# A written list of steps in place of a clock: the order of recurrence and attention in a hybrid diffusion block

## The chip, the cores and the metric

One core of a Trainium2 chip runs one launch of the kernel. The metric is the device time of that launch in microseconds (us); for the kernel before, the median of three runs is 1243.65 us (1242.34 to 1245.85). Five engines matter below: TensorE (PE), VectorE (DVE), ScalarE (ACT), SyncE (SP, which issues the DMAs here) and GpSimd (POOL, nearly unused). Each works through its own instructions in order.

## The reference

One layer over 256 latent and 256 context tokens, 2048 wide, all in float32. Cut to what matters here:

```python
u_x = split_in((rmsnorm(x, norm_w) * (1 + sc_x) + sh_x) @ w_in)      # 10,048 columns; ctx likewise
r, v, kk, decay, a, k_mod = rwkv_prepare(...)                         # per token, two directions, 16 heads of 64

def rwkv7_step(S, xs):                                                # over 256 ctx tokens, then 256 latent ones
    r, w, k, v, kk, akk = xs
    sa = jnp.einsum("dbhij,dbhj->dbhi", S, -kk)
    S = S * w[..., None, :] + sa[..., :, None] * akk[..., None, :] + v[..., :, None] * k[..., None, :]
    return S, jnp.einsum("dbhij,dbhj->dbhi", S, r)

o_rw_x = rwkv_finish(...)                                             # group norm, bonus, silu gate
att_x = blocked_attend(q_x, concat([k_x, k_c]), concat([v_x, v_c]))   # 8 heads, 512 keys, softmax
o_ml_x = att_x * jax.nn.silu(zm_x)
x_new = x + g_x * ((g_r * (o_rw_x @ w_branch_rwkv) + g_m * (o_ml_x @ w_branch_mla)) @ w_out)
```

## The kernel before, in words

**Stages.** First the modulation and the normalised inputs, held for the whole kernel as two halves `hmh` and `hml` (a float32 number as a rounded part and its rest). Then the *recurrence*: the 16 heads are taken as 8 pairs `p`; every pair has a context half and a latent half, so 16 halves, worked in 9 groups of one or two. The 512 tokens are cut into chunks of 64. Then the *attention* over four pairs of heads, then the two branch projections and the output projection.

**Filler.** The projections of `w_in` that the recurrence does not need at once (merge gates, attention's q, k, v, gates, later pairs' columns) are *filler*: `background()` gives them out in pieces. A piece of one weight block loads 256 KB (`w`, by SP, four buffers), rounds it on ACT (`wh`, a CAST of 128x512), takes the rest on DVE (`wl`, a TENSOR_TENSOR of 128x512) and multiplies both into the PSUM tile `acc`: for the 256 latent tokens 12 matmuls per piece, for all 512 tokens a piece is half a block. `wh` has three buffers, `wl` two.

**Chains.** Beside the filler run four kinds of generators, which stop at each `yield`:
- the front chain (`unit_keys`, `front`, `front2`): decays, keys, and the chunk matrices `AQ` and `AR`;
- one `diagonal` per half, the lane that inverts the 16x16 diagonal blocks: `AQ` goes to DRAM (`dl`), comes back in another layout (`ln`, a DMA), is copied to `wt`, inverted there by 14 pairs of instructions on DVE (`pr`, `wt`), goes out to `dw` and comes back as `WT`;
- the back chain (`back`): four rounds of block products (`lev`, PSUM tile `lv`) that make `W2`, then four steps over the chunks, each of three bursts on PE with a copy by DVE or ACT after each: `px` (copied to `xs`), `pu` (copied to `UV`), and the state's update `pm` (`Mn`);
- `final`: group norm, bonus and gate of a finished pair.

**Who sets the order.** `drive` calls the next generator by a clock: the wrappers `Tensor` and `Elementwise` add up an estimate of each instruction's time, and a chain goes on when its estimated results are there (`LF`, `FX`, and the five waits `LT` of a lane) and PE's estimated load over the last `WIN` is at least `DENS`; where no chain is due, a piece of filler comes. In the attention a loop over six stages advances all generators in turn and adds `BG0` = 8 pieces of filler per round in the first stage and `BGM` = 1.3 later. The instructions in that order are then given to a list scheduler, which orders each engine's queue by that order and by priorities: `HP` for the rounding of weights, `HS` for the inversion, `HB` for the tail of a burst on PE.

**Stores.** Finished projections are copied or activated into an SBUF tile `th` and stored to DRAM by SP (`thd`, `zmd`, `kvd`, `qdd`, `krd`), 50 of them, on the queue that also issues the weight loads.

Of the kernel before, what the change touches and what calls it, by code (L numbers as in the profile page):

```python
# [53 lines left out]
HP, HS, HB = 500, 300, 600  # L54
# [3 lines left out]
LF = 0.4  # L58
LATX = 0.0
FX = 2.0  # L60
LT = (3.5, 5.0, 2.0, 4.5, 5.5)
PD = CH * CH + CH

WIN, DENS = 3.0, 0.7
M1 = 24

BG0, BGM = 8, 1.3


class Clock:  # L70

    def __init__(self):
        self.t = 0.0
        self.ready = 0.0
        self.log = []

    def density(self, window):

        while self.log and self.log[0][0] < self.t - window:
            self.log.pop(0)
        return sum(c for _, c in self.log) / window / 1000


class Tensor:


    def __init__(self, engine, clock):
        self.engine, self.clock = engine, clock  # L90

    def add(self, us, columns):
        c = self.clock
        c.t = c.ready = c.t + us
        c.log.append((c.t, columns))
# [10 lines left out]
    def matmul(self, out, lhsT, rhs, **kw):  # L106
        n, k, m = math.prod(rhs.shape[1:]), lhsT.shape[0], math.prod(lhsT.shape[1:])
        if lhsT.dtype == F32R:
            self.add((max(256, n) / 2400 + 0.003) * k / 128, n * k / 128)
        elif m <= 64:  # L110
            self.add(n / 1200 + 0.044, 2 * n * k / 128)
        else:
            self.add((max(512, 4 * n) / 2400 + 0.005) * max(k, 64) / 128, 2 * n * k / 128)
        if self.head is None:
            return self.engine.matmul(out, lhsT=lhsT, rhs=rhs, **kw)  # L115
        if len(self.head) < self.heads:
            self.head.append(self.engine.matmul(out, lhsT=lhsT, rhs=rhs, **kw))  # L117
            return self.head[-1]
        with self.tc.high_priority(HB):
            i = self.engine.matmul(out, lhsT=lhsT, rhs=rhs, **kw)  # L120
            for h in self.head:
                self.tc.add_manual_dep(i.ins, h.ins.name, BEHIND, reason="burst")
        return i

    def transpose(self, *a):
        self.add(0.13, 0)
        return self.engine.transpose(*a)  # L127


class Elementwise:  # L130


    def __init__(self, engine, clock, rate, fixed):
        self.engine, self.clock, self.rate, self.fixed, self.t = engine, clock, rate, fixed, 0.0

    def __getattr__(self, name):
        fn = getattr(self.engine, name)

        def call(out, *a, **kw):
            c = self.clock  # L140
            c.ready = self.t = max(self.t, c.ready) + math.prod(out.shape[1:]) / self.rate + self.fixed
            return fn(out, *a, **kw)  # L142
        return call
# [3 lines left out]
def hybrid_block(  # L147
# [20 lines left out]
    nc = tc.nc  # L168
    clock = Clock()
    V, S = Elementwise(nc.vector, clock, 960, 0.066), Elementwise(nc.scalar, clock, 1200, 0.08)  # L170
    E = Tensor(nc.tensor, clock)
# [300 lines left out]
    def merge_gate_g(i):  # L472

        ps = yield from proj_g(40 + i, T)
        th = wp.tile([P, T], F32, name="th", tag="th", bufs=2)
        S.activation(th, ps, AF.Tanh, scale=0.5)
        nc.sync.dma_start(thd[i], th)
# [8 lines left out]
    def zm_g(i):  # L486

        ps = yield from proj_g(16 + i, T)
        th = wp.tile([P, T], F32, name="th", tag="th", bufs=2)
        S.activation(th, ps, AF.Tanh, scale=0.5)  # L490
        V.scalar_tensor_tensor(th, th, 1.0, ps, ALU.add, ALU.mult)
        nc.sync.dma_start(zmd[i], th)
        done.add(("zm", i))
# [3 lines left out]
    def spill(dst, ps, col):  # L497

        th = wp.tile([P, T], F32, name="th", tag="th", bufs=2)
        n = dst.shape[0]  # L500
        S.copy(th[0:n], ps)
        nc.sync.dma_start(dst, th[0:n])
        sq = wp.tile([P, T], F32, name="th", tag="th", bufs=2)
        S.activation(sq[0:n], ps, AF.Square)
        yield
        pss = pp.tile([P, 512], F32, name="wk", tag="wk", bufs=2)
        for i in range(2):
            E.matmul(pss[:, 2 * i:2 * i + 2], lhsT=sq[0:n, 128 * i:128 * i + 128], rhs=con("ones")[0:n, 0:2], start=True, stop=True)
        V.tensor_copy(sqd[:, col:col + 4], pss[:, 0:4])
# [34 lines left out]
    def run(g, n=1):  # L544
        for _ in range(n):
            if g is not None and next(g, "end") == "end":
                return None
        return g

    def drive(chains, *queues, dens=0.0, lf=1.0, lat=0.0):  # L550

        clock.t = clock.ready = V.t = S.t = 0.0
        chains = [[g, 0.0, None, l] for g, l in chains]
        while chains or any(queues):
            for q in queues:
                if q and not any(c[0] is q[0] for c in chains):
                    chains.append([q[0], clock.t, None, lambda: lf])
            for c in chains:  # L560
                if c[2] is not None and c[2]():
                    c[2] = None
                    c[1] = max(c[1], clock.t)
                if c[2] is None and clock.t >= c[1] and (clock.density(WIN) >= dens or not extra):
                    clock.ready = clock.t
                    r = next(c[0], "end")
                    if r == "end":
                        chains.remove(c)
                        for q in queues:
                            if q and c[0] is q[0]:  # L570
                                q.pop(0)
                    else:
                        c[1] = clock.t + c[3]() * (clock.ready - clock.t) + lat
                        if callable(r):
                            c[2] = r
                        else:
                            c[1] += r or 0.0
                    break
            else:
                t = clock.ready = clock.t  # L580
                next(bg, None)
                if clock.t == t:
                    clock.t += 0.2
# [12 lines left out]
    with tc.tile_pool(name="rw", bufs=1) as rw:  # L596
# [96 lines left out]
        def front(h, k, mi, rho):  # L693
# [81 lines left out]

            yield FX

# [96 lines left out]
        def diagonal(group, AQ, WT, dw):  # L874
# [4 lines left out]
            yield LT[0]  # L879
            ln = rw.tile([64, 16, 16], F32, name="ln", tag="ln")  # L880
            nc.sync.dma_start(ln, blocks(dl))
            yield LT[1]
            with tc.high_priority(HS):
                wt = rw.tile([64, 2, 16, 16], F32, name="wt")
                X = wt[:, 0]
                V.tensor_copy(X[0:32], ln[0:32])
                V.tensor_copy(X[32:64], ln[32:64].rearrange("p r c -> p c r"))
                pr = rw.tile([64, 16, 16], F32, name="pr", tag="ln")
                for k in range(14, 0, -1):

                    m = 15 - k
                    V.tensor_tensor(pr[:, 0:k, 0:m], X[:, 0:k, k:k + 1].to_broadcast([64, k, m]),
                                    X[:, k, k + 1:16].unsqueeze(1).to_broadcast([64, k, m]), ALU.mult)
                    V.tensor_tensor(X[:, 0:k, k + 1:16], X[:, 0:k, k + 1:16], pr[:, 0:k, 0:m], ALU.add)
                V.memset(X.rearrange("p r c -> p (r c)")[:, 0:256:17], 1.0)
                S.copy(wt[:, 1], X.rearrange("p r c -> p c r"))
            yield LT[2]
            for w in range(2):
                nc.sync.dma_start(blocks(dw[w]), wt[:, w])
            yield LT[3]  # L900
# [4 lines left out]
            yield LT[4]  # L905
# [7 lines left out]
        def back(hs_, UV, rho):  # L913
# [45 lines left out]
            for p, lat, Q, AQ, AR, BKT in mem:  # L959
                for g in range(2):  # L960
                    copies[g](AQ[hss[g], g].rearrange("p (d c) t -> p d c t", d=2), Q[hss[g], :, :, 0])
# [35 lines left out]
            for s in range(4):  # L997
# [46 lines left out]
                if lm is not None:  # L1044
                    AR = mem[lm][4]
# [14 lines left out]
        def final(p, Y):  # L1060
# [29 lines left out]
            V.tensor_scalar(y, y, vec("lnw", p), vec("lnb", p), ALU.mult, ALU.add)  # L1090
# [71 lines left out]
        drive([(back_chain(), lambda: LF), (front_chain(), lambda: LF if backs else 1.0)], finals, lanes, dens=DENS, lf=LF, lat=LATX)  # L1162
# [9 lines left out]
    with tc.tile_pool(name="ml", bufs=2) as ml:  # L1172
# [61 lines left out]
        def down():  # L1234
# [24 lines left out]
            split(qdr, qnh, qnl)  # L1259

# [7 lines left out]

            kr2 = ml.tile([P, 4, 2, 64], F32, name="kr2", tag="Pm")
# [12 lines left out]
        def up(hp):  # L1282
# [49 lines left out]
            for h in range(2):  # L1332
                ps = spread(rq[:, 4 + h:12:2])
# [3 lines left out]

            qT, qrT = halfs(ml, [P, 2, T], "qT"), halfs(ml, [P, 2, T], "qrT")
# [96 lines left out]
        due = 0.0  # L1435
        for stage in range(6):
            us = [down()] if stage == 0 else [up(stage - 1)] if stage < 5 else []
            at = [attend(stage - 2)] if stage > 1 else []
            gs = us + at + ([bring()] if stage == 1 else [])
            while gs:  # L1440
                gs = [g for g in gs if run(g) is not None]
                due += BGM if stage else BG0
                while due >= 1:
                    due -= 1
                    next(bg, None)
# [185 lines left out]
```

## Time and profile before

| | |
|---|---|
| runs, median (lowest to highest) | 1243.65 us (1242.34 to 1245.85) |
| the profiled execution's own time | 1251.79 us |
| its span, first to last instruction | 1250.0 us |
| mean granted TensorE clock | 0.990 |
| busy: PE / DVE / ACT | 1191.2 / 936.7 / 596.6 us |
| stages of the span, read from the trace | start to 135 us, recurrence 135 to 872, attention 872 to 1100, rest to 1250 |

A busy PE is not a PE at its peak, since the ends of matmuls are modelled. The chain of waits, followed back from the end, says which engine's work the end waited for at each moment; the table of windows gives each engine's busy time in a stage. All elementwise instructions of DVE and ACT stand under one line, L142 (the wrapper), and the matmuls under L115, L117 and L120, so they are told apart by their tiles.

### The profile page before, as it was taken

The page shows a single profiled execution, that of the slowest core. Times are in us where ns is not written, and L with a number is a line of the kernel's source. Part 1 is how long each engine was busy: PE and PEld are TensorE (multiplying, and loading weights), DVE is VectorE, ACT ScalarE, POOL GpSimd, SP SyncE. Part 2 cuts the span into 40 slices and gives each one's busy share as a digit, 9 for nine tenths or more (in the row PEclk, how much of TensorE's full clock was granted, in tenths as well). Part 3 has the DMA queues.
Part 4 walks back from the last instruction along what each step waited for, and adds up shares of the span by engine and source line. Part 5 has one row for each costly group of instructions (what it writes and reads, how often), then busy time and mean ns, then how long its engine had stood idle before and what let it go on. Part 6 is the DMA issues. An engine that isn't in the chain of part 4 may idle for free.

```text
span 1250.0 us, 30096 instructions
## 1 busy us (share of the span) xinstructions
PE 1191.2 (95%) x11613; PEld 1003.0 (80%) x11613; DVE 936.7 (75%) x2642; ACT 596.6 (48%) x1244; POOL 1.0 (0%) x8
## 2 busy tenths in 40 slices
PE   5999998998999999999999999999999999999998
PEld 2656787787877777878887788789889999999887
DVE  4444676869898888888998888866867767759655
ACT  3434553444454454544545355444555656445443
POOL 0000000000000000000000000000000000000000
PEclk9999999999999999999999999999989999999999
DMA  9999546655464454545652655444854434679774
GB/s 374 339 336 357 180 138 174 165 148 154 123 168 125 117 137 130 157 124 127 158 141 73 169 146 149 131 116 143 265 159 148 135 110 122 185 256 307 242 254 140
DMA packets 213840, 222.53 MB, mean 178 GB/s; under 512 B 112881, under 2 KB 138113, under 8 KB 213185
## 3 DMA queue, kind: packets, MB, share of 16 engines
q1 hardware_dynamic: 213696, 220.61, 58.9%
q8 instruction: 91, 1.49, 0.5%
q14 instruction: 53, 0.43, 0.1%
HBM read 202.59 MB, written 19.03 MB: 177 GB/s over the span
## 4 chain that ended last, share of the span: by engine, by line
PE 64%; DVE 16%; DMA 15%; issue 3%; ACT 2%; SPq 1%; DVEq 0%; ACTq 0%
PE acc L120 25%; PE chp L115 9%; PE lv L115 6%; PE acc L117 5%; DVE wl L142 4%; DMA wm<-in_w_mod_ss 4%; PE a L115 4%; PE ch L115 3%; DMA w<-in_w_proj 3%; PE wk L115 2%; PE wk L127 2%; PE wk L120 2%; DVE wt L142 2%; DMA ln<-dl 2%; PE acc L115 1%
## 5 line engine op out<-in xcount | busy, mean ns | idle before, releaser
L142 ACT CAST wh<-w 128x512 fp32r<-128x512 f32 (+1 forms) x484 | 290.7, 607 | 327.1 <-PE acc L120 118.4
L142 DVE TENSOR_TENSOR wl<-w,wh 128x512 fp32r<-128x512 f32 (+1 forms) x480 | 322.5, 675 | 143.2 <-ACT wh L142 71.6
L120 PE MATMUL acc<-hmh,wl 128*128 128x256 f32 (+1 forms) x1312 | 395.9, 302 | 3.9 <-DVE wl L142 3.8
L120 PE MATMUL acc<-hml,wh 128*128 128x256 f32 (+1 forms) x1312 | 393.7, 300 | 0.0
L120 PE MATMUL acc<-hmh,wh 128*128 128x256 f32 (+1 forms) x928 | 273.3, 294 | 0.0
L120 PEld LDWEIGHTS acc<-hmh,wl 128*128 128x128 f32 x1312 | 247.8, 189 | 17.7 <-DVE wl L142 6.7
L120 PEld LDWEIGHTS acc<-hml,wh 128*128 128x128 f32 x1312 | 248.3, 189 | 8.9 <-issue 1.0
L120 PEld LDWEIGHTS acc<-hmh,wh 128*128 128x128 f32 x928 | 175.4, 189 | 5.0
L117 PE MATMUL acc<-hmh,wh 128*128 128x256 f32 (+1 forms) x384 | 145.7, 379 | 2.5 <-ACT wh L142 1.6
L117 PEld LDWEIGHTS acc<-hmh,wh 128*128 128x128 f32 x384 | 72.4, 189 | 29.0 <-issue 11.7
L142 DVE TENSOR_TENSOR pr<-wt 64x14 f32<-64x14 f32 (+6 forms) x224 | 42.5, 190 | 2.5
L142 DVE TENSOR_TENSOR wt<-wt,pr 64x14 f32<-64x14 f32 (+6 forms) x224 | 42.4, 189 | 2.3
L115 PE MATMUL a<-hmh,wh 128*128 128x512 f32 x96 | 41.5, 432 | 0.0
L115 PE MATMUL pm<-wm,ssil 128*32 128x256 f32 x512 | 34.5, 392 | 5.3 <-DMA wm<-in_w_mod_ss 5.3
L115 PE MATMUL a<-hmh,wl 128*128 128x512 f32 x96 | 38.9, 405 | 0.4 <-DVE wl L142 0.4
L115 PE MATMUL a<-hml,wh 128*128 128x512 f32 x96 | 38.8, 404 | 0.0
L115 PE MATMUL chp<-obh,wh 128*128 128x256 f32 x128 | 36.3, 284 | 0.0
L115 PE MATMUL chp<-obl,wh 128*128 128x256 f32 x128 | 36.2, 283 | 0.0
L115 PE MATMUL chp<-obh,wl 128*128 128x256 f32 x128 | 36.2, 283 | 0.0
L142 ACT ACTIVATE hx<-hx,mod 128x256 f32<-128x256 f32 x32 | 17.5, 594 | 39.0 <-DVE mod L142 39.0
L142 DVE TENSOR_TENSOR hml<-hx,hmh 128x512 fp32r<-128x512 f32 x16 | 11.1, 692 | 29.0 <-ACT hmh L142 29.0
L115 PEld LDWEIGHTS pm<-wm,ssil 128*32 128x32 f32 x512 | 13.9, 110 | 23.4 <-DMA wm<-in_w_mod_ss 10.6
(346 smaller groups left out, 2233.2 us busy)
## 6 DMA issues: line engine op xcount, KB each, us to landing
w<-in_w_proj SPq DMA_DIRECT2D x296, 256.0 KB, 3.0
wm<-in_w_mod_ss SPq DMA_DIRECT2D x64, 512.0 KB, 7.3
w<-in_w_mod_g SPq DMA_DIRECT2D x64, 256.0 KB, 3.3
w<-in_w_br SPq DMA_DIRECT2D x64, 256.0 KB, 3.8
w<-in_w_out SPq DMA_DIRECT2D x64, 256.0 KB, 3.6
WT<-dw SPq DMA_DIRECT2D x32, 256.0 KB, 4.7
w<-in_w_first SPq DMA_DIRECT2D x32, 192.0 KB, 4.8
thd<-th SPq DMA_DIRECT2D x48, 128.0 KB, 2.9
```

The source lines that it names most:

```text
L115: return self.engine.matmul(out, lhsT=lhsT, rhs=rhs, **kw)
L117: self.head.append(self.engine.matmul(out, lhsT=lhsT, rhs=rhs, **kw))
L120: i = self.engine.matmul(out, lhsT=lhsT, rhs=rhs, **kw)
L127: return self.engine.transpose(*a)
L142: return fn(out, *a, **kw)
```

## The change

`drive` and its clock are gone, and the wrappers `Clock` and `Elementwise` with it. `follow` walks a written string: a letter is a chain (`b` back, `f` front, `d` the first lane in the queue, `y` the first `final`), `w` a piece of filler, a number a repetition. A chain that isn't ready at its letter is tried again after each further step. `ORDER` holds 194 `f`, 185 `b`, 112 `d`, 48 `y` and 369 `w`; `BESIDE` orders the attention (`u` preparation, `a` attention, `r` loads of the recurrence's output) with 109 `w`. Five `yield`s are added (one in `back`, two in `down`, one per head and one more in `up`). The priorities are now `HP` 100 (500 before), `HS` 500 (300), `HB` 300 (600). The values that the filler and chains compute are the same.

Moved between engines: the 32 copies of `ln` into `wt` and the 16 copies of `Q` into `AQ` that DVE made go to ACT, as do the 8 scale-and-shift instructions in `final`; the 50 stores of projections go from SP's queue to ACT's. The numbers of all other instructions are unchanged on each engine.

The first place is ACT in the middle of the recurrence, near a back chain's block products and its first step (`AQ`, `ZN`, `UV`, `Y` belong to the back chain, `wh` to the filler, `wt` to a lane). Before:

```order
L142 COPY AQ<-QR 64x512
L142 COPY AQ<-Qc 64x512
L142 COPY ZN<-Z 64x512
L142 CAST wh<-w 128x512
L142 COPY ZN<-Z 64x512
L142 ACTIVATE cv<-acc,vv 128x512
L142 CAST wh<-w 128x512 x2
L142 COPY UV<-chp 64x2x2x64
```

and now:

```order
L911 COPY AQ<-QR 64x512 x2
L911 COPY AQ<-Qc 64x512
L892 COPY ZN<-Z 64x512 x2
L911 COPY AQ<-Qc 64x512
L182 CAST wh<-w 128x512
L225 ACTIVATE cv<-acc,vv 128x512
L182 CAST wh<-w 128x512
L836 COPY wt<-ln 32x256
L837 COPY wt<-ln 32x256
L182 CAST wh<-w 128x512
L975 COPY UV<-chp 64x2x2x64
```

Two more copies of `AQ` and both copies of `ln` have come to this engine; three copies of `AQ` now stand ahead of the first `ZN`, where two did.

The second place is SP from the last `WT` of the recurrence on (`dw` and `WT` belong to a lane, `orwd` is the recurrence's output, `in_gains` the first load of the attention). Before:

```order
L903 DMA WT_1361<-dw_1363 64x16x64 x2
L502 DMA krd<-th 64x256
L237 DMA w<-in_w_proj 128x512 x3
L502 DMA krd<-th 64x256
L237 DMA w<-in_w_proj 128x512 x2
L502 DMA qdd<-th 128x256
L237 DMA w<-in_w_proj 128x512 x3
L1093 DMA orwd<-y 128x256
```

and now:

```order
L849 DMA dw_1363<-wt 64x16x16 x2
L199 DMA w<-in_w_proj 128x512
L853 DMA WT_1361<-dw_1363 64x16x64 x2
L199 DMA w<-in_w_proj 128x512 x8
L1045 DMA orwd<-y 128x256
L199 DMA w<-in_w_proj 128x512 x19
L1045 DMA orwd<-y 128x256
L199 DMA w<-in_w_proj 128x512 x2
L1126 DMA gb<-in_gains 128x256
```

The stores between the weight loads are gone. Counted over the whole queue, 226 loads of filler weights (`w_proj` and `w_kr`) stand ahead of the last `WT` now and 219 before; between it and `in_gains` 29 and 27; behind `in_gains` 43 and 52.

The diff, cut to its core:

```diff
-HP, HS, HB = 500, 300, 600
+HP, HS, HB = 100, 500, 300
-LF = 0.4
-FX = 2.0
-LT = (3.5, 5.0, 2.0, 4.5, 5.5)
-WIN, DENS = 3.0, 0.7
-BG0, BGM = 8, 1.3
+ORDER = (
+    "b f2 w f w2 f w5 f w3 f w8 f w f d w f2 w2 f d w2 f w2 f2 w d w5 f d w3 d2 w4 d b w2 b f w b w b f b w2 b f d w b f w f w b d f "
...
+BESIDE = (
+    "a u w8 u3 w8 u w8 u r2 w u r w2 u w u r w u r w u r w u w r u w r w u3 w u w r u w r u w r w r w2 r w r w r w r w2 r w u a w2 u "
...
-    V, S = Elementwise(nc.vector, clock, 960, 0.066), Elementwise(nc.scalar, clock, 1200, 0.08)
-    E = Tensor(nc.tensor, clock)
+    V, S = nc.vector, nc.scalar
+    E = Tensor(nc.tensor)
...
-        nc.sync.dma_start(thd[i], th)
+        nc.scalar.dma_start(thd[i], th)
...
-        nc.sync.dma_start(zmd[i], th)
+        nc.scalar.dma_start(zmd[i], th)
...
-        nc.sync.dma_start(dst, th[0:n])
+        nc.scalar.dma_start(dst, th[0:n])
...
+    def follow(order, chains, queues):
+        waits = {}
+        def step(c):
+            gs = queues[c] if c in queues else chains[c]
+            if not gs or (gs[0] in waits and not waits[gs[0]]()):
+                return False
+            g = gs[0]
+            waits.pop(g, None)
+            r = next(g, "end")
+            if r == "end":
+                gs.pop(0)
+            elif callable(r):
+                waits[g] = r
+            return True
+        late = []
+        for c, n in re.findall(r"([a-z])([0-9]*)", order):
+            for _ in range(int(n or 1)):
+                if c == "w":
+                    next(bg, None)
+                elif not step(c):
+                    late.append(c)
+                late = [c for c in late if not step(c)]
...
-                V.tensor_copy(X[0:32], ln[0:32])
-                V.tensor_copy(X[32:64], ln[32:64].rearrange("p r c -> p c r"))
+                S.copy(X[0:32], ln[0:32])
+                S.copy(X[32:64], ln[32:64].rearrange("p r c -> p c r"))
...
-                    copies[g](AQ[hss[g], g].rearrange("p (d c) t -> p d c t", d=2), Q[hss[g], :, :, 0])
+                    S.copy(AQ[hss[g], g].rearrange("p (d c) t -> p d c t", d=2), Q[hss[g], :, :, 0])
...
-            V.tensor_scalar(y, y, vec("lnw", p), vec("lnb", p), ALU.mult, ALU.add)
+            S.activation(y, y, AF.Identity, scale=vec("lnw", p), bias=vec("lnb", p))
...
-        drive([(back_chain(), lambda: LF), (front_chain(), lambda: LF if backs else 1.0)], finals, lanes, dens=DENS, lf=LF, lat=LATX)
+        follow(ORDER, {"b": [back_chain()], "f": [front_chain()]}, {"y": finals, "d": lanes})
...
-        due = 0.0
-        for stage in range(6):
...
+        follow(BESIDE, {"u": [up_chain()], "a": [attend_chain()], "r": [bring()]}, {})
```

More of the change, by code (lines that the diff above doesn't have):

```diff
@@ L2 @@
 import math
+import re
 from contextlib import ExitStack, contextmanager
@@ L53, with __init__ @@
 NW, NSP, NSL, NWL, NSX, NWU, UN, NWM = 4, 3, 2, 8, 4, 4, 2, 11
-HP, HS, HB = 500, 300, 600
+HP, HS, HB = 100, 500, 300
 BEHIND = mybir.DependencyInfo(mybir.DependencyClass.NoSync, mybir.DependencyReason.DATA)
-LF = 0.4
-LATX = 0.0
-FX = 2.0
-LT = (3.5, 5.0, 2.0, 4.5, 5.5)
 PD = CH * CH + CH
-WIN, DENS = 3.0, 0.7
-M1 = 24
-BG0, BGM = 8, 1.3
[L70 to L83, printed above, removed]
-class Tensor:
[L89 to L95, printed above, removed]
+ORDER = (
[12 rows of a table added]
+BESIDE = (
[3 rows of a table added]
+M1 = 24
+class Tensor:
+    def __init__(self, engine):
+        self.engine, self.transpose = engine, engine.transpose
     head = None
@@ L106, in matmul @@
     def matmul(self, out, lhsT, rhs, **kw):
[L107 to L113, printed above, removed]
         if self.head is None:
@@ L123, in matmul @@
         return i
[L125 to L143, printed above, removed]
 @with_exitstack
@@ L168, in hybrid_block @@
     nc = tc.nc
-    clock = Clock()
-    V, S = Elementwise(nc.vector, clock, 960, 0.066), Elementwise(nc.scalar, clock, 1200, 0.08)
-    E = Tensor(nc.tensor, clock)
+    V, S = nc.vector, nc.scalar
+    E = Tensor(nc.tensor)
     PSUM = bass.MemoryType.PSUM
@@ L542, in kr_g @@
             yield from spill(krd[:, ts], ps[0:64, ts], 16 + 4 * j)
[L544 to L580, printed above, removed]
@@ new lines, in follow @@
+    def follow(order, chains, queues):
[20 more added lines that the diff above has]
+                late = [c for c in late if not step(c)]
+        while any(chains.values()) or any(queues.values()):
+            if not any([step(c) for c in [*chains, *queues]]):
@@ L581, in drive @@
                 next(bg, None)
-                if clock.t == t:
-                    clock.t += 0.2
     def silu_gate(dst, ps, tmp):
@@ L774, in front @@
                 V.tensor_tensor(Q[:, :, :, 1], dirs(cr), ecols(Ep, 1, 0), ALU.mult)
-            yield FX
+            yield
             AQ = rw.tile([P, 2, 8, CH], F32, name="AQ", bufs=4)
@@ L878, in diagonal @@
                 nc.sync.dma_start(dl[:, g, 0:CH * CH].rearrange("u (r c) -> r u c", c=CH), AQ[hss[g], g])
-            yield LT[0]
+            yield
             ln = rw.tile([64, 16, 16], F32, name="ln", tag="ln")
             nc.sync.dma_start(ln, blocks(dl))
-            yield LT[1]
+            yield
             with tc.high_priority(HS):
@@ L896, in diagonal @@
                 S.copy(wt[:, 1], X.rearrange("p r c -> p c r"))
-            yield LT[2]
+            yield
             for w in range(2):
                 nc.sync.dma_start(blocks(dw[w]), wt[:, w])
-            yield LT[3]
+            yield
             yield lambda: levels >= group
@@ L904, in diagonal @@
                                   dw[:, :, g, 0:CH * CH].rearrange("w u (r c) -> r (w u) c", c=CH))
-            yield LT[4]
+            yield
             nonlocal inverted
@@ L1044, in back @@
                 if lm is not None:
+                    if ms:
+                        yield
                     AR = mem[lm][4]
@@ L1259, in down @@
             split(qdr, qnh, qnl)
+            yield
             pt = wk()
@@ L1267, in down @@
                 rope(krr[:, i:i + 1], kr[:, i:i + 1], i, 1)
+            yield
             kr2 = ml.tile([P, 4, 2, 64], F32, name="kr2", tag="Pm")
@@ L1332, in up @@
             for h in range(2):
+                yield
                 ps = spread(rq[:, 4 + h:12:2])
@@ L1335, in up @@
                 S.copy(rkb[h], ps)
+            yield
             qT, qrT = halfs(ml, [P, 2, T], "qT"), halfs(ml, [P, 2, T], "qrT")
@@ L1433, in hybrid_block, with up_chain, attend_chain @@
         closing = True
-        due = 0.0
-        for stage in range(6):
[L1437 to L1445, printed above, removed]
+        attended = 0
+        def up_chain():
+            yield from down()
+            for p in range(4):
+                yield lambda: attended >= p - 1
+                yield from up(p)
+        def attend_chain():
+            nonlocal attended
+            for p in range(4):
+                yield lambda: p in ups
+                yield from attend(p)
+                attended += 1
+        follow(BESIDE, {"u": [up_chain()], "a": [attend_chain()], "r": [bring()]}, {})
     mg = ctx.enter_context(tc.tile_pool(name="mg", bufs=2))
```

13 rows, old and new, of tables (BESIDE, ORDER) are left out of this document.

## The prediction

> **What bounds the kernel now.** I read the page's first and fourth parts, then the windows of the three stages that the change can reach, then the chain of waits inside the recurrence.
>
> ```profile
> span 1250.0 us, 30096 instructions
> PE 1191.2 (95%) x11613; PEld 1003.0 (80%) x11613; DVE 936.7 (75%) x2642; ACT 596.6 (48%) x1244; POOL 1.0 (0%) x8
> ...
> PE 64%; DVE 16%; DMA 15%; issue 3%; ACT 2%; SPq 1%; DVEq 0%; ACTq 0%
> ```
>
> PE looks 95% busy, but the end waited for PE only 64% of the time; 16% of the span, 200 us, it waited for DVE, 15% for DMAs. The windows (PE, PEld, DVE, ACT, POOL, clock, DMA share, GB/s):
>
> ```profile
> 135.00:872.00 737.00, 707.52 (x8287) 595.34 (x8286) 611.56 (x1842) 348.06 (x753) 0.43 (x2) 1.00 0.52 140
> 872.00:1100.00 228.00, 222.69 (x1615) 207.35 (x1614) 167.95 (x444) 127.17 (x269) 0.21 (x1) 0.98 0.53 164
> 1000.00:1050.00 50.00, 50.00 (x358) 46.46 (x359) 36.05 (x105) 27.21 (x60) 0.00 (x0) 1.00 0.35 109
> ```
>
> The recurrence takes 737 us. DVE is busy for 83% of it (611.56), ACT for 47% (348.06). In the attention PE hardly lets go: from 1000 to 1050 it is busy for all 50 us at full clock. The first 135 us and the tail after the attention hold the same program in both kernels. So what can be won lies in the recurrence, and the chain of waits for its window says where:
>
> ```profile
> by line: PE acc L120 30.8%; PE chp L115 8.2%; PE acc L117 7.1%; DVE wl L142 6.1%; DMA w<-in_w_proj 3.8%; PE wk L120 3.2%; issue 3.0%; DVE wt L142 2.9%; DMA ln<-dl 2.9%; PE acc L115 2.5%; PE wk L115 2.4%; PE wk L127 2.1%; PE lv L120 2.0%; DV
> ...
> 430.89 1.30 PE acc L120 x11
> ...
> 433.70 0.30 DVE UV L142
> 434.89 0.68 DVE wl L142
> 435.80 0.44 DVE UV L142
> 436.57 0.42 DVE gacc L142
> 437.28 0.68 DVE wl L142
> 438.19 0.43 DVE UV L142
> ```
>
> The five groups of it that are not PE's add up to 6.1 + 3.8 + 3.0 + 2.9 + 2.9 = 18.7% of 737, 138 us. The pieces show how: from 433.7 to 438.6 the chain runs through DVE from one copy to the next, because a copy that the back chain needs stands behind roundings in DVE's queue. And one burst of filler, 12 matmuls, is 1.30 us for 11 of them, so 1.40.
>
> **The change, part by part**, against the profiled execution's 1251.8 us.
>
> *A. Work off DVE.*
>
> ```profile
> L142 DVE COPY AQ<-Qc x8: 420/422/424, 215.1 to 787.1; 64x512 f32<-64x512 f32 x8
> L142 DVE COPY AQ<-QR x8: 424/424/425, 295.7 to 829.1; 64x512 f32<-64x512 f32 x8
> L142 ACT COPY AQ<-Qc x8: 612/617/622, 212.6 to 785.1; 64x512 f32<-64x512 f32 x8
> ...
> L142 DVE COPY wt<-ln 32x256 f32<-32x256 f32 x32 | 10.5, 327 | 4.9 <-DMA ln<-dl 4.5
> L142 ACT COPY wt<-wt 64x256 f32<-64x256 f32 x16 | 10.3, 642 | 10.6 <-DVE wt L142 10.6
> ...
> L142 DVE TENSOR_SCALAR y<-y,vv x8: 399/411/415, 356.5 to 871.0; 128x256 f32<-128x256 f32 x8
> L142 ACT ACTIVATE ysq<-y x8: 417/418/422, 347.4 to 864.0; 128x256 f32<-128x256 f32 x8
> ```
>
> 16 x 0.423 = 6.8, 32 x 0.327 = 10.5 and 8 x 0.411 = 3.3: 20.6 us leave DVE, all in the recurrence, 3.4% of its 611.56 there. The most this gives is 20.6, if every freed slot lets a waiting copy through; the least is what DVE's share of the chain says, 200 of 936.7 busy us or 21% of it, 4.3. I take **-10**, about half: DVE's queue is long where these copies stand (beside the block products and the inversion), which is nearer to the upper end than the average is.
>
> *B. The same work on ACT, and the stores' issue.* AQ: 16 x 0.617 = 9.9. The copies of `ln` have no row on ACT; they lie between DVE's 0.327 and ACT's 0.642 for a copy of `wt` with twice the partitions, so 10.5 to 20.5. The scale and shift go by `ysq`, 8 x 0.418 = 3.3. The stores' issue is known only on SP:
>
> ```profile
> L477 SPq DMA_DIRECT2D thd<-th x32: 326/327/1615, 192.9 to 1037.7; - x32
> L502 SPq DMA_DIRECT2D qdd<-th x4: 384/424/1068, 826.0 to 865.8; - x4
> ...
> SPq L477 <- ACT th L142: 14.9, 19, 4.2
> SPq L502 <- ACT th L142: 13.3, 6, 4.6
> ```
>
> 50 x 0.327 is 16.4, some 34 of them (24 `thd`, 10 others) in the recurrence, 11. Together 35 to 45 us come to ACT there: 348 becomes about 388 of 737, 53%. That is covered by ACT's idle half, and ACT is on 2% of the chain. What isn't covered is order: three `AQ` copies now stand ahead of `ZN`, where two did, and the second block product waits for `ZN`; 0.62 us in each of the seven groups with two halves is 4.3. If nothing of the rest is covered it costs up to 45. I take **+5**.
>
> *C. Stores out of SP's queue.* The two rows of waits above, 28 us, are time in which SP stood at a store whose data wasn't ready, with weight loads queued behind it. They go. Of the loads, 3.8% of 737 = 28 us is on the chain. At best all 28 are gone; at worst nothing, since with four buffers most loads wait for `wl` to free one:
>
> ```profile
> SPq L237 <- DVE wl L142: 357.9, 231, 5.8
> ```
>
> 28 of some 386 us of these waits is 7%; but a store's wait stops loads whose buffer is free, so I take **-5**, between 7% of 28 and all of it. The Trainium skill (DMA: Bandwidth & Descriptors, Issuing engines are not separate DMA queues) says that issuing from several engines saves only the sequencer's time to issue. By that rule this term is zero and the sum below 5 us higher; the trace speaks against it in part, since 28 us of SP's time here is waiting and not issuing, and no run shows yet which decides.
>
> *D. Filler moved into the recurrence.* By the queue of SP, seven more pieces stand ahead of the last `WT` (226 for 219). A piece costs PE 1.40; taken out of the stages where PE is busy throughout, seven give 9.8. Put into the recurrence they cost nothing where PE waits for a chain, and their roundings cost DVE 7 x 0.686 = 4.8 there:
>
> ```profile
> L142 DVE TENSOR_TENSOR wl<-w,wh 128x512 fp32r<-128x512 f32 x238 | 163.1, 686 | 50.9 <-PE acc L120 23.2 <-ACT wh L142 12.5 <-issue 10.5
> ```
>
> Between -9.8 and 0 (if the recurrence is as long by them); **-7**.
>
> *E. The list itself.* The number of instructions on PE doesn't change. The planner's gaps between chain steps go, the inversion (`HS`) now outranks roundings, the finer steps let filler in between block products and in the attention's preparation, where PE is idle for 228.0 - 222.7 = 5.3 us. No row prices it. If it lets filler cover a quarter of the 138 us, it gives 35; if the list mistimes its steps as often as the clock did and adds a wait of one burst, 1.4 us, at half of the 36 chunk steps, it costs 25. The ends lie nearly even about zero; the regular spacing of the list leans to a gain: **-7**.
>
> Sum: -10 + 5 - 5 - 7 - 7 = **-24**, so 1227.8 for an execution like the profiled one. The runs' median stands 0.65% below it (1243.65 to 1251.79); the same share off gives 1219.8, and I say **1220 us**. Its own range runs from 1203 (A whole, D whole, E -10: -40) to 1237 (A -4.3, C and E nothing: -6).
>
> **The rivals.**
>
> *ACT becomes the gate (slower).* The copies of `ln` now wait for their DMA at the head of ACT's queue, and behind them stand the roundings `wh` and the copies `UV`, without which PE has neither filler nor a next step.
>
> ```profile
> L881 SPq DMA_DIRECT2D ln<-dl x16: 597/603/1123, 173.6 to 793.3; - x16
> ...
> DMA to landing us min/median/max: 2.7/3.3/4.9
> ```
>
> If ACT comes to them as the load is issued, it is held for 3.3 plus the two copies (0.65 to 1.28), 4.0 to 4.6 us. Two rounded pieces (`wl` has two buffers) cover 2 x 1.40 = 2.8; the rest, 1.2 to 1.8, is lost 16 times: 19 to 29. With 34 stores x 0.327 = 11 and the 4.3 at `ZN` that is 34 to 44, against A and D, -17: +22 at the middle, 1273.8, and by the median's share **1265**. It decides from the point where ACT is held for more than 2.8 us. For it: in the chain's row above `ln` is 2.9%, 21 us, already. Against it: on DVE the same copies waited only 4.5 us in all, so the load has mostly landed by then.
>
> *Nothing that can be told.* PE's work is the same and fills the time however the others are arranged; A, C and D fall where something else is late too. For it: PE's 707.5 busy of 737. Against it: the 138 us. Time **1243**, within 0.3% (3.7 us), about what can be told from no change here.
>
> *The list covers much more.* Half of the 138 us go: 1251.8 - 69 = 1182.8, with the median's share **1175**. For it: the chain's pieces are short waits, each covered by one burst in the right place. Against it: DVE at 611.6 - 20.6 + 4.8 = 596 busy would then fill 89% of a recurrence of 668 us.
>
> **How the numbers follow.** Forecast 0.63, ACT as the gate 0.15, no difference 0.10, much more 0.12. The forecast's range and the last rival are faster by over 0.3%: 0.75; same 0.10; slower 0.15. For 8 in 10 the range reaches from 1192 to 1250: it leaves out most of the last rival (0.09) and of the gate (0.11).
>
> **What would show it.** DVE's busy time in the recurrence down to about 596, with the stage shorter by 15 to 25 us; A and E right if DVE's `UV` and `wl` fall in the chain of waits. C: the loads' 3.8% falls, and no row shows ACT waiting long behind a store. D: the stages behind the recurrence are shorter by about 10 us. B wrong, and the gate right, if ACT's row of `wt<-ln` shows tens of us of waiting for the DMA, and `wh` then stands ahead of PE. The forecast is wrong altogether if the recurrence isn't shorter than 730 us, or if DVE keeps its 83% there while PE's share of the chain doesn't rise.

## The result and the profile after

| | before | after |
|---|---|---|
| runs, median (lowest to highest) | 1244.24 us (1242.34 to 1245.85) | 1222.99 us (1220.15 to 1225.42) |
| the profiled execution's own time | 1251.79 us | 1225.42 us |
| its span | 1250.0 us | 1223.6 us |

The median of before counts a fourth run beside the three ahead of the prediction. The ratio of the times is 0.9829, with a 95% interval of 0.9802 to 0.9855: 21 us less. The forecast was 1220.

The page of the changed kernel, its first part and the shares of its chain of waits:

```profile
span 1223.6 us, 30064 instructions
PE 1172.8 (96%) x11613; PEld 995.4 (81%) x11613; DVE 922.7 (75%) x2586; ACT 625.7 (51%) x1300; POOL 1.0 (0%) x8
...
PE 73%; DMA 12%; DVE 10%; ACT 3%; issue 2%; SPq 0%; DVEq 0%; ACTq 0%
```

DVE has 56 instructions fewer, ACT 56 more, PE the same 11613. The stage borders of the prediction were rough. For a comparison the span is cut at five landmarks that both kernels have: the first filler matmul, the last `AR` matmul of the back chain, the first matmul that prepares queries, the last matmul of the attention's output, the last matmul of filler. Windows of before, then of after (us, PE, PEld, DVE, ACT, POOL, clock, DMA share, GB/s):

```profile
138.70:861.00 722.30, 692.82 (x8181) 581.83 (x8180) 601.07 (x1813) 339.29 (x736) 0.00 (x0) 1.00 0.52 140
861.00:892.20 31.20, 29.99 (x242) 28.03 (x237) 24.76 (x72) 15.59 (x30) 0.21 (x1) 1.00 0.70 220
892.20:1082.40 190.20, 188.43 (x1354) 175.68 (x1353) 139.87 (x379) 109.12 (x237) 0.00 (x0) 0.98 0.47 144
1082.40:1111.40 29.00, 26.67 (x208) 25.82 (x207) 16.84 (x28) 11.65 (x19) 0.00 (x0) 0.94 0.77 242
1111.40:1250.00 138.60, 133.86 (x770) 118.00 (x769) 93.72 (x177) 63.92 (x110) 0.00 (x0) 1.00 0.75 241
```

```profile
136.10:854.70 718.60, 695.17 (x8281) 592.11 (x8280) 594.25 (x1768) 373.96 (x802) 0.00 (x0) 0.99 0.52 144
854.70:889.80 35.10, 32.76 (x262) 30.47 (x258) 26.61 (x74) 17.59 (x33) 0.20 (x1) 1.00 0.72 236
889.80:1070.00 180.20, 179.99 (x1318) 168.39 (x1317) 136.61 (x377) 106.21 (x231) 0.00 (x0) 1.00 0.47 148
1070.00:1085.60 15.60, 14.58 (x123) 14.10 (x122) 10.56 (x18) 7.34 (x12) 0.00 (x0) 1.00 0.81 251
1085.60:1223.60 138.00, 133.64 (x771) 118.06 (x769) 94.22 (x177) 63.66 (x110) 0.00 (x0) 1.00 0.74 244
```

By stage: start -2.6, recurrence -3.7, the bridge to the attention +3.9, attention -10.0, filler behind the attention -13.4, rest -0.6; together -26.4. About 6 of it belong to the granted clock of the two executions: its mean was 0.990 before and 0.995 after (1250.0 x 0.010 less 1223.6 x 0.005 is 6.4). Most of that lies in the third and fourth windows of before, at 0.98 and 0.94 (190.2 x 0.02 + 29.0 x 0.06 = 5.5). The medians differ by 21.

The recurrence, at which the change is aimed, is hardly shorter. But it holds more. The same windows for the filler's tile `acc` alone (us, PE, PEld, DVE, ACT, ...), the recurrence and the filler behind the attention, of before:

```profile
138.70:861.00 722.30, 487.73 (x3048) 386.08 (x3048) 42.76 (x82) 31.09 (x72) 1.00 0.52 140
...
1082.40:1111.40 29.00, 26.59 (x204) 25.79 (x204) 3.35 (x8) 0.00 (x0) 0.94 0.77 242
```

and of after:

```profile
136.10:854.70 718.60, 498.00 (x3144) 399.68 (x3144) 43.41 (x83) 32.20 (x75) 0.99 0.52 144
...
1070.00:1085.60 15.60, 14.39 (x119) 14.07 (x120) 1.74 (x5) 0.00 (x0) 1.00 0.81 251
```

96 matmuls of filler more, eight pieces of 12, at the 1.40 us of a piece 11 us of PE, were done in a recurrence that is 3.7 us shorter. They are missing where PE is busy throughout: 85 fewer behind the attention, and the attention too has 36 fewer PE instructions (1354 and 1318). So most of the gain was made in the recurrence and is seen behind it.

### The profile page after: what moved, and what is told of

Its sections match the earlier page's. It is cut to its first block, busy times and chain, and to the rows that moved or that the text cites. A ratio compares the mean times of both kernels' runs of the same rounds, so it can differ in the third digit from the quotient of the medians.

```text
span 1223.6 us, 30064 instructions
## 1 busy us (share of the span) xinstructions
PE 1172.8 (96%) x11613; PEld 995.4 (81%) x11613; DVE 922.7 (75%) x2586; ACT 625.7 (51%) x1300; POOL 1.0 (0%) x8
## 4 chain that ended last, share of the span: by engine, by line
PE 73%; DMA 12%; DVE 10%; ACT 3%; issue 2%; SPq 0%; DVEq 0%; ACTq 0%
PE acc L103 28%; PE chp L98 12%; PE lv L98 7%; PE acc L100 5%; DMA wm<-in_w_mod_ss 4%; PE a L98 4%; PE ch L98 4%; DVE wl L183 3%; DMA w<-in_w_proj 2%; PE wk L98 2%; PE wk L103 2%; DMA ln<-dl 2%; PE lv L103 1%; PE acc L98 1%; PE wk L100 1%
## 5 line engine op out<-in xcount | busy, mean ns | idle before, releaser
L842 DVE TENSOR_TENSOR pr<-wt 64x14 f32<-64x14 f32 (+6 forms) x224 | 42.8, 191 | 16.8 <-ACT wt L837 13.8
```

## The experiments

All kernels below do the same computation. Ratios are to runs of the kernel before that were taken in the same round, whose medians lay from 1245.75 to 1247.39 us, with 95% intervals. The *moves* are the part of the change that puts copies, scale-and-shift and stores on ACT; the *list* is `ORDER`, `BESIDE`, `follow` and the finer steps; the *priorities* are `HP, HS, HB`.

**The moves alone.** The kernel before with

```diff
-        nc.sync.dma_start(thd[i], th)
+        nc.scalar.dma_start(thd[i], th)
...
-                V.tensor_copy(X[0:32], ln[0:32])
-                V.tensor_copy(X[32:64], ln[32:64].rearrange("p r c -> p c r"))
+                S.copy(X[0:32], ln[0:32])
+                S.copy(X[32:64], ln[32:64].rearrange("p r c -> p c r"))
```

and the same for `zmd`, `dst`, `AQ` and the scale-and-shift. The clock stays, and plans with the copies' time on ACT.

> The kernel before with its clock, and only the moves between engines: the copies of AQ and of ln and the scale and shift go to ACT, the 50 stores to ACT's queue. The prediction's terms A, B and C: -10 + 5 - 5, so 10 us less than before, about 1234. Rival, the list does it all (DVE and SP were off the path): 1244, no difference. Rival, ACT as the gate: slower than before, 1250 or more, with tens of us of ACT waiting at the copies of ln.

Measured: 1255.07 us, 1.0082 (1.0052 to 1.0112). The moves by themselves make this kernel slower, by 10 us.

**The list with the priorities, without the moves.** The changed kernel with those lines turned back, so with the list, the finer steps and the new priorities.

> The changed kernel with every move undone: DVE makes the copies and the scale and shift again, SP issues the stores; the list, the finer steps and the priorities stay. The prediction's terms D and E: -14, about 1230 to 1233, some 9 us over the changed kernel. Rival, the list does it all: 1223, as the changed kernel. Rival, the list needs the free DVE (its filler in the recurrence costs DVE 4.8 us more): 1240 or more.

Measured: 1231.77 us, 0.9891 (0.9861 to 0.9921). So on top of the list the same moves are worth 0.9829 - 0.9891, -0.6%, where on the clock they cost 0.8%. Windows of the recurrence in this kernel:

```profile
136.80:866.70 729.90, 702.21 (x8269) 592.43 (x8268) 609.35 (x1822) 342.51 (x746) 0.00 (x0) 0.99 0.52 141
```

With nearly as many PE instructions as the changed kernel (8269 and 8281) the stage is 11.3 us longer, and DVE is busy 15 us longer (609.35 and 594.25). What the moves bring on the list, they bring in this stage. The list without them did not shorten it: against before it takes 88 PE instructions more (8181 to 8269, 10.3 us at 1.40 per 12) and is 7.6 us longer (722.30 to 729.90), so much of that filler was paid for with time there.

**The stores alone.** The changed kernel with the 50 stores back on SP:

```diff
-        nc.scalar.dma_start(thd[i], th)
+        nc.sync.dma_start(thd[i], th)
```

and the other two stores likewise.

> The changed kernel with only the 50 stores put back on SP's queue. The prediction's term C: 5 us slower than the changed kernel, 1228, with some 28 us of SP waiting at the stores again. By the skill's rule that another issuing engine saves only the time to issue: no difference, 1223.

Measured: 1227.36 us, 0.9865 (0.9832 to 0.9898). The queue of SP waits at the stores again, in total us, times, longest:

```profile
SPq L439 <- ACT th L438: 26.5, 19, 4.7
...
SPq L464 <- ACT th L466: 9.8, 5, 3.7
```

36 us of such waits come back, and the time moves by 0.36%, 4.4 us, with intervals that overlap. The sign is likely, not shown. The loads' own waits for `wl` to free a buffer change the other way. With the stores on SP, and then in the changed kernel:

```profile
SPq L199 <- DVE wl L183: 367.5, 229, 6.2
```

```profile
SPq L199 <- DVE wl L183: 411.5, 240, 7.9
```

So the 36 us at the stores turn up, in the changed kernel, as 44 us more of waiting for a buffer. That is how a move of the stores can be worth little.

**The attention's list alone.** The kernel before with `follow(BESIDE, ...)` and the finer steps of `up` and `down`, its recurrence still by the clock.

```diff
-        due = 0.0
-        for stage in range(6):
...
+        follow(BESIDE, {"u": [up_chain()], "a": [attend_chain()], "r": [bring()]}, {})
```

> The kernel before with its clock in the recurrence, and only the attention by the written list BESIDE with its finer steps. The trace of the changed kernel is 10.0 us shorter from the first matmul of the query preparation to the last of the attention, with 4.2 us less filler in it, and 13.3 shorter behind it, with 9.9 us less filler. If the list and the finer steps cover waits in the attention: 5 to 9 us faster than before, 1235 to 1239. If the gain there is only filler that the recurrence took over: 1244, no difference.

Measured: 1246.85 us, 1.0007 (0.9986 to 1.0028): nothing that can be told. The attention of the changed kernel was shorter by 10.0 us. Of these the 36 PE instructions that were done before it are 4.2, and the clock of before's execution there, 0.98 for 1.00, is 3.8. Whether the attention's list brings something behind the recurrence's list was not run.

**The moves with the plan kept.** In the first experiment the clock plans anew, since it now counts the moved work on ACT. Here a wrapper (`Moved`) issues it on ACT and counts it at DVE's rate on DVE's clock, so that the plan stays nearly that of before and mainly the engines differ:

```diff
+    SV = Moved(nc.scalar, V)
...
-                V.tensor_copy(X[0:32], ln[0:32])
+                SV.copy(X[0:32], ln[0:32])
```

> As the kernel before with the moves alone (1.0082 of before, slower), but the clock still counts the moved copies as DVE's, so that it plans nearly the order of before (on PE 1263 lines of difference to before, where the moves alone had 5993 to this one). If the moves alone lost because the clock planned another order: 8 to 10 us faster than before, 1236 to 1238, what the same moves gave on the list (0.9829 against 0.9891). If ACT's queue became the gate under the old priorities: 1250 or more again.

Measured: 1252.55 us, 1.0058 (1.0038 to 1.0077). So the moves cost on the clock with the old plan too; the new plan is not the main reason. The recurrence's window:

```profile
134.40:865.70 731.30, 695.50 (x8181) 584.88 (x8180) 586.35 (x1758) 369.56 (x791) 0.00 (x0) 0.99 0.52 138
```

The filler is the same as before (8181 PE instructions), DVE has 15 us less to do (601.07 to 586.35), and the stage is 9 us longer (some of it may be the clock, 0.99 for 1.00; the medians say 7). The waits in the recurrence (136 to 860) show one place where the freed time went:

```profile
DVE pr L142 <- ACT wt L159: 15.7, 11, 3.2
...
ACT wt L159 <- DMA ln<-dl: 6.6, 7, 1.5
```

The inversion (`pr`) on DVE now waits 15.7 us in total for ACT's copy of `ln` into `wt` (L159 is the wrapper that issues it on ACT). That is about the length of the copies themselves: in the changed kernel's trace the two copies of a lane take 404 and 640 ns on ACT, 16.7 us for 16 lanes. There this wait is nearly as long, 13.8 us; so it isn't what tells the two apart. What tells them apart stays open.

**The priorities.** Three kernels with this one line: the changed kernel with the old values, the kernel before with the new ones, and the kernel of the last experiment with the new ones. The line for the first; the other two have it the other way round:

```diff
-HP, HS, HB = 100, 500, 300
+HP, HS, HB = 500, 300, 600
```

> The changed kernel with the old priorities (HP 500, HS 300, HB 600). The prediction gave them no price of their own within its term E of -7. If they are a small part: 1223 to 1227. If the moved copies need them (roundings at 500 stand ahead of the inversion's copies on ACT): 1233 or more.

Measured: 1240.28 us, 0.9930 (0.9905 to 0.9955). The old priorities take back more than half of the gain.

> The kernel before with only the new priorities (HP 100, HS 500, HB 300). On the list with the moves they were worth 0.9829 against 0.9930, 12 to 14 us. If they carry over to the clock: 1232 to 1236. If they only suit the list: 1244 or more, as before or slower.

Measured: 1246.99 us, 1.0004 (0.9987 to 1.0020). On the clock they are worth nothing.

> The kernel before with its clock, the moves (counted by the clock as DVE's, so that its plan stays) and the new priorities: all of the change but the list and the finer steps. If the list adds nothing: 1223, as the changed kernel. If moves and priorities need each other but the list adds its share (about half of the 21 us): 1233. If without the list they are worth nothing: 1244 to 1252.

Measured: 1250.50 us, 1.0038 (1.0019 to 1.0058). With the moves on the clock, they do not make these a gain either.

**The last corner**: the list with finer steps, without moves, with the old priorities.

> Only the list and the finer steps: no move, the old priorities. With the new priorities this was 0.9891 of before. If the list alone is what counts: 1231 to 1234. If priorities are worth the same here as with the moves (0.0101): 1244, no difference to before.

Measured: 1236.45 us, 0.9928 (0.9907 to 0.9949). With it all eight corners are measured:

| | neither | priorities | moves | both |
|---|---|---|---|---|
| clock | 1 | 1.0004 | 1.0058 | 1.0038 |
| list | 0.9928 | 0.9891 | 0.9930 | 0.9829 |

The list alone gives 0.7%, 9 us. Priorities and moves together give another 1.0%, 12 us, on the list, and cost 0.4% on the clock. Moves without the new priorities are worth nothing on the list (0.9928 and 0.9930); priorities without the moves 0.4%, which is at the edge of what the intervals tell. That moves and priorities gain more together than each by itself on the list, 0.9829 where the single steps give 0.9893, stands only just outside the noise: 0.64%, where the four intervals together leave about 0.5% (an estimate from their widths). The three priorities were changed together, so no run shows which of them does it.

**One copy back.** The changed kernel with the second, transposing copy of `ln` on DVE again.

```diff
-                S.copy(X[32:64], ln[32:64].rearrange("p r c -> p c r"))
+                V.tensor_copy(X[32:64], ln[32:64].rearrange("p r c -> p c r"))
```

> The changed kernel with the second copy of ln (columns and rows exchanged, 640 ns on ACT) back on DVE, so that both copies run side by side. In the changed kernel's trace DVE waits 13.8 us for that copy. If these waits are on the path: up to 10 us faster than the changed kernel, 1213 to 1218. If the relief of DVE is worth more than them: slower by up to 5 us, 1223 to 1228. A list that suits only the instructions that it was written for would make it slower by more.

Measured: 1228.52 us, 0.9857 (0.9832 to 0.9882), 0.3% behind the changed kernel with overlapping intervals. The page of its profiled execution says something else of use:

```profile
PE 64%; DVE 15%; DMA 14%; issue 3%; ACT 3%; SPq 0%; ACTq 0%; DVEq 0%
```

That execution's span was 1223.7 us, as long as the changed kernel's 1223.6. But PE's share of the chain is 64% and not 73%. So this share alone does not follow the time. Nor do the rows of single lines; the chain in its recurrence (136 to 855) begins:

```profile
by line: PE acc L103 29.2%; PE chp L98 8.2%; PE acc L100 6.7%; DVE wl L183 5.5%; DMA w<-in_w_proj 4.7%; issue 4.6%; PE wk L103 3.4%; DMA ln<-dl 3.0%; PE acc L98 2.1%; PE lv L103 2.0%; DVE pr L842 2.0%; PE wk L98 2.0%; DVE wt L844 1.9%; PE w
```

**The amount of filler.** The changed kernel with 12 of the 365 `w` ahead of the last `b` taken out of `ORDER`, and with 12 added, both spread evenly; the filler left over or lacking is done later. The first edits of the one and the other:

```diff
-    "b f2 w f w2 f w5 f w3 f w8 f w f d w f2 w2 f d w2 f w2 f2 w d w5 f d w3 d2 w4 d b w2 b f w b w b f b w2 b f d w ...
+    "b f2 w f w2 f w5 f w3 f w7 f w f d w f2 w2 f d w2 f w2 f2 w d w5 f d w3 d2 w4 d b w2 b f w b w b f b w b f d w ...
```

```diff
-    "b f2 w f w2 f w5 f w3 f w8 f w f d w f2 w2 f d w2 f w2 f2 w d w5 f d w3 d2 w4 d b w2 b f w b w b f b w2 b f d w ...
+    "b f2 w f w2 f w5 f w3 f w9 f w f d w f2 w2 f d w2 f w2 f2 w d w5 f d w3 d2 w4 d b w2 b f w b w b f b w3 b f d w ...
```

> The changed kernel with 12 of the 365 pieces of filler taken out of the list ahead of the last back step, evenly; they come later. The prediction's term D: filler in the recurrence is free, so 12 x 1.40 = 17 us slower, 1240. If the recurrence is as much shorter as its filler (no wait left for it to cover): no difference, 1223. Between them by the list alone, whose recurrence grew by 7.7 us with 9.9 us more filler: 4 us slower, 1227.

Measured: 1261.14 us, 1.0102 (1.0073 to 1.0131).

> The changed kernel with 12 more pieces of filler in the list, evenly. By term D: up to 17 us faster, 1206, until nothing is left to move. If the recurrence has no more waits to give: 1223 or a little slower, since DVE gets 12 x 0.686 = 8 us more there.

Measured: 1250.62 us, 1.0031 (1.0007 to 1.0054).

Against the changed kernel that is +2.8% and +2.1%: either way the whole gain is gone. The recurrence with 12 pieces fewer:

```profile
135.00:880.20 745.20, 708.01 (x8193) 593.22 (x8192) 587.85 (x1759) 370.06 (x792) 0.00 (x0) 0.98 0.51 136
```

and with 12 more:

```profile
134.30:888.10 753.80, 718.76 (x8351) 609.85 (x8352) 599.48 (x1775) 378.23 (x809) 0.00 (x0) 0.98 0.53 139
```

With 88 PE instructions fewer than in the changed kernel (8281) the stage is 26.6 us longer; with 70 more, 35.2 longer, where those 70 at 1.40 per 12 are 8.2. So the 12 letters moved about 7 and 6 pieces of 12 matmuls across the end of the stage. The clock in both windows is 0.98 where the changed kernel's was 0.99, which is some 7 us of each, and the profiled execution with 12 more took 1258.67 us, 8 over its median.

The letters of the chains stand in the same sequence in all three strings, but the order on PE is not the same. Of the 5120 matmuls of the back and front chains in the traces (matched by their tiles and their count) 413 stand out of the changed kernel's order with 12 pieces fewer and 265 with 12 more, against 86 in the list without the moves. The lag behind the changed kernel, read along the `pu` bursts, grows with 12 more from 5.6 us at the first to 34 at the last; with 12 fewer it reaches 25, and shrinks now and then on the way. What makes it stays open: what ends a task of filler (the copy to `th`, a convolution, a store) may fall beside other chain steps, or a chain that waits for a projection may come to its step later, or the scheduler may order the chains another way. No run separates these.

No kernel of these beats the changed one.

## Why the prediction was right, and where it was not

The total was right: 1223 for 1220, -24 forecast for the profiled execution, -26 found. In part that was luck. The terms hold along one order of taking the parts only, the list first: taken first, on the clock, the moves cost 7 us (1.0058) where -10 was forecast for them, and everything else then brings 28. And the priorities, on which the moves' gain hangs, stood in the sum without a price.

*D and E, list, steps and priorities: -14 forecast, 1.1% or 13.6 us measured* (0.9891, the list without the moves). In the changed kernel the eight pieces moved into the recurrence (seven forecast) cost it no time; the stages behind it are shorter by 10.0 + 13.4 - 3.9 = 19.5 us, where 10 were forecast: 11 of them the pieces, 5 the clock of before's execution. But D put the free time down to the list, and the list without the moves had to pay for much of it: its recurrence was 7.6 us longer for 10.3 us of them. And with 12 letters fewer the time rose by twice the 17 us that D's price gave, and with 12 more it rose too. E did not come in full by the way that it named, either. It was priced as gaps covered; of its parts the attention's list with its finer steps brought nothing under the clock's recurrence (1.0007), and the priorities, which got no price of their own, bring 12 us when they meet both list and moves and none on the clock.

*A, B and C, the moves: -10 forecast, 0.6% or 7.7 us measured on the list* (0.9891 to 0.9829). **The step that failed is A's**: that a freed slot on DVE "lets a waiting copy through" by itself, which put -10 into the sum with no condition, and the test that went with it, a recurrence shorter by 15 to 25 us. DVE's time came down by less than was said: 15.8 us in the recurrence were forecast (20.6 less 4.8), and it fell by 6.8 (601.07 to 594.25). The moves alone took 15 off it, on the clock (601.07 to 586.35) and on the list (609.35 to 594.25), where the rows of the moved work add up to 20; the list put 8 on (601.07 to 609.35). DVE kept its 83% of the stage: 83.2% before, 82.7% after. And on the clock the freed slots, under nearly the same plan, made the kernel 0.6% slower; on the list with the old priorities they were worth nothing. On the list the moves became a gain only with the new priorities, which among other things let the inversion go ahead of roundings. The recurrence came out only 3.7 us shorter: with the 11 us of filler that it took in, 15 us were gained there, but they appear as shorter stages behind it. In the range for A, "the least is what DVE's share of the chain says, 4.3" was no lower bound: it left out a loss, which the clock's corner shows.

*B's sizes were right, but for one row.* ACT is busy 35 us more in the recurrence (339.29 to 373.96). In that are 5 us of roundings for the eight pieces (8 x 0.607), so 30 for the moved work, where 24 to 34 were forecast without the stores. Issues of DMAs do not count as busy: the 35 stores of the stage took 12 us of ACT's time beside it, where 11 were forecast. Together that is 42, inside B's 35 to 45. What this work cost in time, forecast as +5, no run shows by itself. The copies of `ln` lie within their bounds and `AQ` has the price of its row. The scale and shift took 602 ns where 418 had been taken from `ysq`:

```profile
L836 ACT COPY wt<-ln x16: 387/404/406, 177.3 to 793.9; 32x256 f32<-32x256 f32 x16
L837 ACT COPY wt<-ln x16: 619/640/652, 177.7 to 794.3; 32x256 f32<-32x256 f32 x16
...
L911 ACT COPY AQ<-Qc x16: 615/618/619, 204.5 to 778.0; 64x512 f32<-64x512 f32 x16
...
L1042 ACT ACTIVATE y<-y,vv x8: 597/602/602, 355.8 to 865.6; 128x256 f32<-128x256 f32 x8
...
L439 ACTq DMA_DIRECT2D thd<-th x32: 326/327/353, 181.4 to 1002.6; - x32
```

*C is not settled.* -5 was forecast, 4.4 us with overlapping intervals were measured. The loads' share of the chain in the recurrence, which should have fallen from 3.8%, is 4.1%:

```profile
by line: PE acc L103 35.2%; PE chp L98 8.9%; PE acc L100 7.8%; DMA w<-in_w_proj 4.1%; DVE wl L183 3.7%; PE wk L103 3.5%; DMA ln<-dl 3.0%; issue 2.7%; PE lv L103 2.5%; PE acc L98 2.5%; PE wk L98 2.3%; PE wk L100 1.9%; ACT wh L182 1.6%; PE wk
```

What fell is `wl`, from 6.1% to 3.7%, with `UV` the sign that the prediction named for A and E; but with one copy back `wl` has 5.5% at the same span, so the sign tells little. The rule of the Trainium skill (DMA: Bandwidth & Descriptors, Issuing engines are not separate DMA queues), by which this term is zero, is therefore neither borne out nor refuted here.

*The rival "ACT becomes the gate" did not come.* Its sign was the row of `wt<-ln`. The waits of the changed kernel in the recurrence (136 to 860):

```profile
ACT wh L182 <- DMA w<-in_w_proj: 71.1, 55, 5.1
...
DVE pr L842 <- ACT wt L837: 13.8, 8, 2.7
...
ACT wt L836 <- DMA ln<-dl: 11.3, 6, 5.0
```

ACT stood 11.3 us at the loads of `ln`, in 6 of 16 cases, where the rival needed ACT to be held each time. On the clock the moves did cost 5 to 10 us, but the traces there show 6.6 and 7.9 us of that wait with the plan kept and 13.2 where the clock planned anew, nowhere the tens of us that the rival needed, so that loss isn't the rival's either. It has no shown cause. The rivals "nothing" and "much more" (1243 and 1175) are both outside what was measured.

*The tests for "wrong altogether" were bad ones.* The first was a recurrence that isn't shorter than 730 us, 7 less than its 737. It came out 3.7 shorter, so by this test the forecast was wrong, while the time was right: the test did not allow for a stage that keeps its length and takes in more work. The second was that DVE keeps its 83% "while PE's share of the chain doesn't rise". DVE kept it; PE's share rose from 64% to 73%, but the experiment with one copy back had 64% at the same span. A likely reason is that the chain follows one release at each step, so that where two things end nearly together a small shift moves whole pieces from one row to the other.

## What to carry to other kernels

An order that is written out, the priorities under it and the engines of the copies can depend on one another: here two parts that were worth nothing or cost time alone gave as much as the third when all came together, so a part of such a change is judged in the company it will have, with the corners measured, not by its own instructions alone. Work moved off a busy engine can be worth less than nothing: the same moves cost 0.6% under one order and gained 0.6% under another. And where independent work fills gaps, count that work stage by stage: a stage that keeps its length and holds more is the gain, and the time for it turns up in later stages.

## What the runs showed of the hardware

A copy of 64x512 float32 took 618 ns on ACT and 422 on DVE. A copy of 32x256 took 404 ns on ACT, and 640 with its last two dimensions exchanged, so the exchange cost ACT some 236 ns (the two also lie on different partitions). On DVE, in the list without the moves, the same two took 281 and 374, so there the exchange cost 93:

```profile
L836 DVE COPY wt<-ln x16: 271/281/282, 176.7 to 806.9; 32x256 f32<-32x256 f32 x16
...
L837 DVE COPY wt<-ln x16: 367/374/393, 177.0 to 807.2; 32x256 f32<-32x256 f32 x16
```

The prediction had DVE's mean of 327 for both, and 642 from another copy as their upper bound on ACT.

What was not expected at all is how sharply the time depends on where the filler stands: 12 letters among 365, 17 us of PE by the forecast's price and 10 and 8 us as they fell, added or taken away cost 25 to 34 us (0.0202 and 0.0273 of 1244).
